# Scattering expert outputs in a two-layer encoder: gate shares by slot, all members summed in one PSUM bank

## The chip, the cores and the metric

One core of a Trainium2 chip runs the whole program. The metric is device time of one execution in microseconds (us). PE is TensorE, DVE VectorE, ACT ScalarE, SP SyncE, which issues the weight transfers.

## The reference

Two post-norm layers over x (256 tokens by 1024). Each has a mixer of three head groups (convolution, differential attention, gated DeltaNet) and a feed-forward part. In layer 1 that part is a mixture of eight experts, of which each token uses two:

```python
logits = t @ router_w
top_v, top_i = lax.top_k(logits, 2)
gates = softmax(top_v)
combine = sum(one_hot(top_i, 8) * gates[..., None], axis=1)
for e in range(8):
    out = out + combine[:, e:e+1] * ((silu(t @ w1[e]) * (t @ w3[e])) @ w2[e])
x = layer_norm(ALPHA * x + out)
```

w1 and w3 of an expert are 1024x3584, w2 is 3584x1024, all in f32.

## The kernel before, in words

**Planner.** The code records instructions, and `Plan.flush` orders each recorded stretch by a list scheduler (`Plan.forward`) with prices of its own. A recorded `E.` operation (class `Either`) goes to ACT, and to DVE only where the planner has ACT busy for more than 6.9 us beyond. After the trunk (everything up to the routing) PE's order is the order of recording (`p.strict`). Each flush ends all engines' lists for that stretch: an instruction of the next stretch stands behind all of this one on its engine. Tiles of one tag have a fixed number of slots, taken in order of recording. ACT and DVE, or PE and either, never touch the same bank and quadrant of PSUM at once: the planner puts a wait between them.

**Experts.** `route` and `places` compute `comb` (the gate shares, token by expert) and `pos` (each token's slot in an expert). Experts are sorted by load into eight places, and `GROUPS` (line 108) makes four groups of them: (0), (2,5), (3,4), (1,6,7). The members' turns over chunks of 512 columns alternate in a group (`TURNS`). In the executions shown each group runs its usual arm, `USUAL_ARMS` (line 113), with so many rows per member: 64; 128 and 64; 128 and 64; 128+64, 32 and 32. A member of 128 rows multiplies in three passes of split operands (fp32r high and low parts of x and of the weights, which ACT casts and DVE subtracts); rows of 64 and 32 ("few") multiply raw f32 in two or four column strips of PE, and their output y lies packed in one bank: strip q of it holds columns q of n of the 1024.

**Weights.** 336 units of 1 MB go through a ring of ten buffers (`RING2`, line 133). SP issues the load of unit u+10 as soon as PE, or the casts, have let unit u go.

**Gather.** `gather` (line 1501) makes one-hot tables `OH` (token by slot) in two blocks of 128 slots, their transposes `oht`, and from them the gathered rows `xe` (16 tiles of 2x128 fp32r columns for each parity of the group). `gather_few` (line 1535) does it for a member of up to 64 rows, into `x64`. The steps for group g+1 are recorded between the turns of group g, one after each turn from the third chunk on (line 1655). Those of group 0 are at the end of the trunk (`before_moe`, line 1673).

**Scatter.** When all turns of a group are done, `Rows.scatter` (line 1860) goes through the members: it splits a bank of y into a high and a low fp32r part (ACT cast, DVE subtraction) in two of the four `mhT` slots, and `Kernel.scatter` (line 1664) multiplies both with the one-hot table of 128 tokens into a bank of tag `pg`, for both token halves t, and adds the bank, times `comb`, into the result `xr` by one DVE instruction. The piece is 512 columns for rows of 128 and of 64, and 256 for rows of 32. So the arms have 4, 8, 8 and 24 such additions. The result of the last group goes straight into `last_norm` (line 1333), on DVE.

**Between groups** each engine takes a branch (`tc.If` on `rare[g]`, line 1723). `HINT` (line 135) puts a mark for the likely next arm so many instructions before the end of each engine's list in the arm: 40 on PE, 10 on ACT, 14 on DVE.

Lines in the profile are nearly all L601 (one place issues all instructions), so groups go by tiles: `bank` is PSUM, `whi`/`wlo`/`parts` are split weights, `xe` or `y` gathered rows, `mhT` the split hidden rows and the split y, `hx` hidden rows of few.

Of the kernel before, what the change touches and what calls it, by code (L numbers as in the profile page):

```python
# [604 lines left out]
class Kernel:  # L605
# [97 lines left out]
    def setup(self, pool):  # L703
# [3 lines left out]
        self.oht = [self.const("oht0", [128, 2, 2, 128], FR)]  # L707
        p.slots("raw", pool, RING, 2048)
# [792 lines left out]
    def gather(self, p, pos, blocks, misc):  # L1501
# [20 lines left out]

        def rows(q, i):
# [8 lines left out]
        return [table] + [lambda q=q, i=i: rows(q, i) for q in range(4) for i in range(2)]  # L1532


    def gather_few(self, p, i, place):
# [13 lines left out]
        def rows():  # L1549
# [6 lines left out]
            self.E.copy(self.x64[p][i], ps)  # L1556

        return [table, rows]

    def gather_group(self, g):  # L1560
# [3 lines left out]
        steps = self.gather(g % 2, self.pos, [(h, C_IOTA), (h, C_IOTA2)], "pg")  # L1564
# [43 lines left out]
    def arm(self, g, *blocks, hint=None):  # L1608
# [8 lines left out]
        if own:  # L1617
            for f in self.gather(1 - p, self.pos, [(GROUPS[g][m], C_IOTA) for m in (own * 2)[:2]], "pg"):
                f()
        members = []  # L1620
        for m, b in enumerate(blocks):
            place = GROUPS[g][m]
            if m and m not in own:
                x, oht = self.x64[p][m - 1], self.oht64[p][m - 1]
                if b == (32,):
                    for r in (32, 96):
                        self.A.copy(oht[r:r + 32], oht[0:32])
                members.append(Rows(self, place, [], [], x[:, :, 0:b[0]], oht))
                continue
            q, at = (1 - p, own.index(m)) if m else (p, 0)  # L1630
            xe, oht = self.xe[q], self.oht[q]
# [3 lines left out]
            if 64 in b:  # L1635
# [4 lines left out]
                few = x, oht[:, n]  # L1640
            members.append(Rows(self, place, xs, ohts, *few))
# [15 lines left out]
        for x in members:  # L1657
            x.scatter()
# [5 lines left out]
    def scatter(self, place, s, oht, y):  # L1664
        for t in range(2):
            ps = self.t("pg", [128, s.stop - s.start])
            self.mm(ps, oht[:, t, :], y[0], True, False)
            self.mm(ps, oht[:, t, :], y[1], False, True)
            self.V.scalar_tensor_tensor(self.xr[:, t, s], ps, self.comb[:, t, place:place + 1], self.xr[:, t, s],
                                        op0=OP.mult, op1=OP.add)  # L1670


    def before_moe(self):
# [10 lines left out]
        for f in self.gather(0, self.slot, [(0, C_IOTA), (0, C_IOTA2)], "pd"):  # L1684
# [3 lines left out]
    def moe(self, pool):  # L1688
        p, nc, tc = self.plan, self.nc, self.tc
        for name, n, words, dt in (("raw2", RING2 - RING, 2048, F32), ("parts", 2, 1024, FR),  # L1690
                                   ("xe", 16, 256, FR), ("oht", 1, 512, FR), ("ohr", 1, 512, FR),
                                   ("mh", 4, 512, F32), ("mhT", 4, 512, FR),
                                   ("td", 8, 16, F32), ("x64", 4, 512, F32), ("oht64", 3, 256, FR),
                                   ("hx", 2, 256, F32)):
# [5 lines left out]
        self.oht.append(self.t("oht", [128, 2, 2, 128], FR, True))  # L1700
# [294 lines left out]
```

## Time and profile before

| | us |
|---|---|
| three runs | 1534.03, 1540.43, 1548.97; median 1540.43 |
| profiled execution | 1527.84 |
| its span, first to last instruction | 1526.1 |
| PE busy | 1414.6 (93%) |
| DVE busy | 822.9 (54%) |
| ACT busy | 585.9 (38%) |
| mean granted PE clock | 0.944 |

The trunk takes the first 628 us; group 0 runs to about 720, group 1 to 955, group 2 to 1186, group 3 to 1512, and the last norm to the end. The clock is a share of 2.4 GHz: 0.50 is 1.2 GHz. A record's duration holds latency; the rate of back-to-back instructions is read from start to start. An f32 matmul leaves two records, an fp32r one of 256 or 512 columns leaves one.

### The profile page before, as it was taken

What the parts mean: (1) busy time and instruction counts of PE and PEld (TensorE: products, weight loads), DVE (VectorE), ACT (ScalarE), POOL (GpSimd) and SP (SyncE); (2) the same over time, 40 slices, a digit from 0 to 9 for tenths busy, and PEclk for the clock granted to TensorE, in tenths of its full rate; (3) what the DMA queues carried; (4) which work ended last, traced back from release to release, by engine and by line L of the source; (5) the groups of instructions that cost most, each with busy time, mean ns of one, the idle gap of its engine ahead of it and who ended that gap; (6) DMA issues with size and microseconds to landing.
All of it is one profiled execution on the core that took longest, in us unless ns stands there. A gap on an engine that the chain in (4) does not pass through costs nothing. (4 is left out here: it accounts for less than half of the span.)

```text
span 1526.1 us, 25192 instructions
## 1 busy us (share of the span) xinstructions
PE 1414.6 (93%) x10040; PEld 1038.4 (68%) x10040; DVE 822.9 (54%) x1669; ACT 585.9 (38%) x969; POOL 16.5 (1%) x33
## 2 busy tenths in 40 slices
PE   8989979999799897898999999999999899999995
PEld 6768769999587676654667666667666666665663
DVE  5995765555769748301555455655454523334346
ACT  4455334444333543211543354444444423323230
POOL 0100000000010000000000000000000000000000
PEclk9988889999899689899899999999999999999997
DMA  8231325455332215599999899899999799999992
GB/s 320 85 136 66 116 100 205 166 193 179 125 111 83 84 56 227 205 421 420 420 420 421 354 373 421 354 413 388 349 372 422 290 420 420 420 420 420 420 419 85
DMA packets 61750, 431.90 MB, mean 283 GB/s; under 512 B 7088, under 2 KB 7856, under 8 KB 10032
## 3 DMA queue, kind: packets, MB, share of 16 engines
q1 hardware_dynamic: 61616, 430.13, 70.4%
q8 instruction: 82, 1.34, 0.4%
q14 instruction: 52, 0.43, 0.1%
HBM read 429.05 MB, written 1.05 MB: 282 GB/s over the span
## 5 line engine op out<-in xcount | busy, mean ns | idle before, releaser
L601 DVE TENSOR_TENSOR wlo<-raw,whi 128x1024 fp32r<-128x1024 f32 x289 | 347.2, 1223 | 356.1 <-ACT whi L601 292.6
L601 ACT CAST whi<-raw 128x1024 fp32r<-128x1024 f32 x289 | 295.7, 1049 | 240.6 <-PE bank L601 196.9
L601 PE MATMUL bank<-raw,x 128*32 128x128 f32 (+1 forms) x3584 | 266.2, 330 | 1.8 <-DVE x L601 1.8
L601 PEld LDWEIGHTS bank<-raw,x 128*32 128x32 f32 (+1 forms) x3584 | 171.2, 124 | 83.8 <-issue 29.6
L601 PE MATMUL bank<-xT,whi 128*128 128x256 f32 x928 | 163.6, 285 | 0.0
L601 PE MATMUL bank<-whi,y 128*128 128x512 f32 x472 | 146.8, 411 | 1.9 <-ACT y L601 0.9
L601 PEld LDWEIGHTS bank<-xT,whi 128*128 128x128 f32 x928 | 138.2, 191 | 5.0 <-ACT L L601 0.8
L601 PE MATMUL bank<-raw,hx 128*64 128x512 f32 (+1 forms) x896 | 131.6, 497 | 0.0
L601 PE MATMUL bank<-whi,xe 128*128 128x512 f32 x336 | 113.0, 418 | 12.2 <-ACT whi L601 9.5
L601 PEld LDWEIGHTS bank<-whi,y 128*128 128x128 f32 x472 | 89.3, 197 | 26.5 <-issue 7.3
L601 PE MATMUL bank<-xT,wlo 128*128 128x256 f32 x464 | 106.3, 285 | 0.8 <-DVE wlo L601 0.8
L601 DVE TENSOR_TENSOR mh<-mh,bank 128x256 f32<-128x256 f32 (+2 forms) x63 | 30.2, 480 | 138.2 <-PE bank L601 138.2
L601 PEld LDWEIGHTS bank<-raw,hx 128*64 128x64 f32 (+1 forms) x896 | 43.7, 125 | 70.3 <-issue 52.0
L601 ACT ACTIVATE mh<-bank 128x256 f32<-128x256 f32 (+2 forms) x63 | 27.2, 432 | 166.1 <-PE bank L601 166.1
L601 PEld LDWEIGHTS bank<-whi,xe 128*128 128x128 f32 x336 | 61.9, 194 | 40.0 <-issue 17.6
L601 PE MATMUL bank<-wlo,y 128*128 128x512 f32 x236 | 85.2, 404 | 3.1 <-DVE wlo L601 3.1
L601 PE MATMUL bank<-whi,mhT 128*128 128x512 f32 x252 | 83.1, 411 | 2.8 <-ACT whi L601 2.8
L601 PE MATMUL bank<-L,raw 128*128 128x256 f32 x352 | 80.5, 386 | 5.4 <-ACT v L601 1.9
L601 PEld LDWEIGHTS bank<-xT,wlo 128*128 128x128 f32 x464 | 78.9, 191 | 3.2 <-DVE wlo L601 1.0
L601 PEld LDWEIGHTS bank<-L,raw 128*128 128x128 f32 x352 | 66.2, 192 | 18.9 <-DVE cpad L601 2.8
L601 DVE TENSOR_TENSOR parts<-raw,parts 128x1024 fp32r<-128x1024 f32 x63 | 76.8, 1218 | 1.7 <-ACT parts L601 1.6
L601 ACT CAST mhT<-bank 128x512 fp32r<-128x512 f32 (+1 forms) x33 | 18.9, 574 | 147.0 <-PE bank L601 146.7
(231 smaller groups left out, 1719.6 us busy)
## 6 DMA issues: line engine op xcount, KB each, us to landing
raw<-in_w SPq DMA_DIRECT2D x400, 1024.0 KB, 10.5
L<-in_row SPq DMA_DIRECT2D x3, 1024.0 KB, 4.6
L<-in_xt SPq DMA_DIRECT2D x2, 512.0 KB, 7.6
raw<-in_w SPq DMA_DIRECT2D x2, 512.0 KB, 8.3
xr<-in_x SPq DMA_DIRECT2D x1, 1024.0 KB, 7.3
raw<-in_row SPq DMA_DIRECT2D x2, 512.0 KB, 7.5
out_y<-xr SPq DMA_DIRECT2D x4, 256.0 KB, 2.1
pw<-in_pw SPq DMA_DIRECT2D x2, 256.0 KB, 4.8
```

What stands on the lines that cost most here:

```text
L601: getattr(self.api[o.eng], o.name)(*[real(x) for x in o.a], **{n: real(x) for n, x in o.k.items()})
```

## The change

The share of a slot (the gate of the token that sits in it) is now computed when the rows are gathered: `shares` multiplies the one-hot table with `comb` into a column, two f32 matmuls of one column for each block, and a DVE copy from PSUM. `gather` gets that as one more step at its end, and `gather_few` does it behind its rows. At the end of a group `Rows.pieces` takes each 256 columns of y times the share (ACT) into a high part and, by one DVE instruction from PSUM, into the low part; both go into the group's own `xe` tiles, which the first products no longer need. `Kernel.scatter` then goes by output piece: four pieces of 256 columns, two token halves, and in each bank all members' high and low products in one accumulation, followed by one DVE addition of 256 columns into `xr`. Each arm so has 8 additions. Where rows of 64 or 32 repeat the one-hot table in other partitions, their shares are copied too (ACT). One slot of tag `td` goes, and `share` tiles come. The diff, whole:

```diff
@@ -705,6 +705,7 @@
         self.pool = pool
         self.slots(pool, True)
         self.oht = [self.const("oht0", [128, 2, 2, 128], FR)]
+        self.share, self.pg = [self.const("share0", [128, 2])], False
         p.slots("raw", pool, RING, 2048)
         self.raws = [self.t("raw", [128, 2048], keep=True) for _ in range(RING)]
         self.xr = self.const("xr", [128, 2, D])
@@ -1498,7 +1499,7 @@
         V.tensor_copy(self.table[:, 2].bitcast(I32), rare)
 
 
-    def gather(self, p, pos, blocks, misc):
+    def gather(self, p, pos, blocks, misc, places):
         A, V, T = self.A, self.V, self.T
         xe, oht = self.xe[p], self.oht[p]
         OH = []
@@ -1520,6 +1521,10 @@
                     T.transpose(pt[:, b, t, :], OH[0][:, t, b, :].bitcast(F32), self.ident)
             A.copy(oht, pt)
 
+        def shares():
+            for b, place in enumerate(places):
+                self.shares(self.share[p][:, b:b + 1], [OH[0][:, t, b, :] for t in range(2)], place)
+
         def rows(q, i):
             ps = self.t(misc, [128, 2, 2, 128])
             for j in range(2):
@@ -1529,7 +1534,7 @@
             for j in range(2):
                 (A.copy if i == 0 else V.tensor_copy)(xe[i][2 * q + j], ps[:, j])
 
-        return [table] + [lambda q=q, i=i: rows(q, i) for q in range(4) for i in range(2)]
+        return [table] + [lambda q=q, i=i: rows(q, i) for q in range(4) for i in range(2)] + [shares]
 
 
     def gather_few(self, p, i, place):
@@ -1554,6 +1559,7 @@
                         self.mm(ps[:, kb, :], self.xh[x][t][:, kb * 128:kb * 128 + 128], OH[0][:, t, 0, :],
                                 kb + t + x == 0, kb + t + x == KB + 1)
             self.E.copy(self.x64[p][i], ps)
+            self.shares(self.share64[p][i], [OH[0][:, t].rearrange("p a b -> p (a b)") for t in range(2)], place)
 
         return [table, rows]
 
@@ -1561,7 +1567,7 @@
         if g >= len(GROUPS):
             return []
         h, *few = GROUPS[g]
-        steps = self.gather(g % 2, self.pos, [(h, C_IOTA), (h, C_IOTA2)], "pg")
+        steps = self.gather(g % 2, self.pos, [(h, C_IOTA), (h, C_IOTA2)], "pg", [h, h])
         for i, place in enumerate(few):
             steps += self.gather_few(g % 2, i, place)
         return steps
@@ -1615,20 +1621,22 @@
         self.psum_tags({"py": ny, "pg": 8 - ny})
         steps, own = self.gather_group(g + 1), [m for m, b in enumerate(blocks) if 128 in b and m]
         if own:
-            for f in self.gather(1 - p, self.pos, [(GROUPS[g][m], C_IOTA) for m in (own * 2)[:2]], "pg"):
+            mine = [GROUPS[g][m] for m in (own * 2)[:2]]
+            for f in self.gather(1 - p, self.pos, [(place, C_IOTA) for place in mine], "pg", mine):
                 f()
         members = []
         for m, b in enumerate(blocks):
-            place = GROUPS[g][m]
             if m and m not in own:
                 x, oht = self.x64[p][m - 1], self.oht64[p][m - 1]
+                share = self.share64[p][m - 1]
                 if b == (32,):
                     for r in (32, 96):
                         self.A.copy(oht[r:r + 32], oht[0:32])
-                members.append(Rows(self, place, [], [], x[:, :, 0:b[0]], oht))
+                        self.A.copy(share[r:r + 32], share[0:32])
+                members.append(Rows(self, [], [], [], x[:, :, 0:b[0]], oht, share))
                 continue
             q, at = (1 - p, own.index(m)) if m else (p, 0)
-            xe, oht = self.xe[q], self.oht[q]
+            xe, oht, share = self.xe[q], self.oht[q], self.share[q]
             full = [at + n for n in range(b.count(128))]
             xs = [lambda kb, n=n, xe=xe: [xe[i][kb][:, n, :] for i in range(2)] for n in full]
             ohts, few = [oht[:, n] for n in full], ()
@@ -1637,8 +1645,9 @@
                 for kb in range(KB):
                     self.V.tensor_tensor(x[:, kb, :], xe[0][kb][:, n, 0:64], xe[1][kb][:, n, 0:64], OP.add)
                 self.A.copy(oht[64:128, n], oht[0:64, n])
-                few = x, oht[:, n]
-            members.append(Rows(self, place, xs, ohts, *few))
+                self.A.copy(share[64:128, n:n + 1], share[0:64, n:n + 1])
+                few = x, oht[:, n], share[:, n:n + 1]
+            members.append(Rows(self, xs, ohts, [share[:, n:n + 1] for n in full], *few))
         alone = len(members) == 1
         for n, (m, k, ch) in enumerate(turns):
 
@@ -1654,20 +1663,34 @@
                 members[m].second(ch)
             if steps and ch >= 2 and not own:
                 steps.pop(0)()
-        for x in members:
-            x.scatter()
+        self.scatter(p, members)
         for f in steps:
             f()
         self.plan.flush(hint)
 
 
-    def scatter(self, place, s, oht, y):
+
+    def scatter(self, p, members):
+        room = [x.rearrange("p a b -> p (a b)") for part in self.xe[p] for x in part]
+        while members:
+            n = next(n for n in range(len(members), 0, -1) if sum(x.tiles() for x in members[:n]) <= len(room))
+            tiles, now, members = iter(room), members[:n], members[n:]
+            found = [y for x in now for y in x.pieces(tiles)]
+            for q in range(4):
+                mine, s = [y[1:] for y in found if y[0] == q], slice(256 * q, 256 * q + 256)
+                for t in range(2):
+                    ps = self.t("pg", [128, 256])
+                    for i, (oht, *parts) in enumerate(mine):
+                        for k, y in enumerate(parts):
+                            self.mm(ps, oht[:, t, :], y, i + k == 0, i == len(mine) - 1 and k == 1)
+                    self.V.tensor_tensor(self.xr[:, t, s], ps, self.xr[:, t, s], OP.add)
+
+
+    def shares(self, out, OH, place):
+        ps = self.t("pg" if self.pg else "pd", [128, 1])
         for t in range(2):
-            ps = self.t("pg", [128, s.stop - s.start])
-            self.mm(ps, oht[:, t, :], y[0], True, False)
-            self.mm(ps, oht[:, t, :], y[1], False, True)
-            self.V.scalar_tensor_tensor(self.xr[:, t, s], ps, self.comb[:, t, place:place + 1], self.xr[:, t, s],
-                                        op0=OP.mult, op1=OP.add)
+            self.mm(ps, OH[t].bitcast(F32), self.comb[:, t, place:place + 1], t == 0, t == 1)
+        self.V.tensor_copy(out, ps)
 
 
     def before_moe(self):
@@ -1681,7 +1704,7 @@
 
             self.E.mul(self.xr[:, t, :], self.xr[:, t, :], ALPHA)
         self.bias("gather")
-        for f in self.gather(0, self.slot, [(0, C_IOTA), (0, C_IOTA2)], "pd"):
+        for f in self.gather(0, self.slot, [(0, C_IOTA), (0, C_IOTA2)], "pd", [0, 0]):
             f()
         self.plan.bias = 0.0
 
@@ -1690,14 +1713,16 @@
         for name, n, words, dt in (("raw2", RING2 - RING, 2048, F32), ("parts", 2, 1024, FR),
                                    ("xe", 16, 256, FR), ("oht", 1, 512, FR), ("ohr", 1, 512, FR),
                                    ("mh", 4, 512, F32), ("mhT", 4, 512, FR),
-                                   ("td", 8, 16, F32), ("x64", 4, 512, F32), ("oht64", 3, 256, FR),
-                                   ("hx", 2, 256, F32)):
+                                   ("td", 7, 16, F32), ("x64", 4, 512, F32), ("oht64", 3, 256, FR),
+                                   ("hx", 2, 256, F32), ("share", 4, 2, F32)):
             p.slots(name, pool, n, words, dt)
         first = [self.raws[u % RING] for u in range(M0, M0 + RING)]
         self.raws2 = first + [self.t("raw2", [128, 2048], keep=True) for _ in range(RING2 - RING)]
         self.parts.append([self.t("parts", [128, 1024], FR, True) for i in "hl"])
         self.xe.append([[self.t("xe", [128, 2, 128], FR, True) for kb in range(KB)] for i in "hl"])
         self.oht.append(self.t("oht", [128, 2, 2, 128], FR, True))
+        self.share.append(self.t("share", [128, 2], keep=True))
+        self.share64, self.pg = [[self.t("share", [128, 1], keep=True) for _ in range(n)] for n in (1, 2)], True
         self.x64 = [[self.t("x64", [128, KB, 64], keep=True) for _ in range(n)] for n in (1, 2)]
         self.oht64 = [[self.t("oht64", [128, 2, 128], FR, True) for _ in range(n)] for n in (1, 2)]
         for u in range(M0 + RING, M0 + RING2):
@@ -1782,8 +1807,9 @@
 
 
 class Rows:
-    def __init__(self, k, place, xs, ohts, few=None, oht_few=None):
-        self.k, self.place, self.xs, self.ohts, self.few, self.oht_few = k, place, xs, ohts, few, oht_few
+    def __init__(self, k, xs, ohts, shares, few=None, oht_few=None, share_few=None):
+        self.k, self.xs, self.ohts, self.shares = k, xs, ohts, shares
+        self.few, self.oht_few, self.share_few = few, oht_few, share_few
         self.ys = [[k.t("py", [128, 512]) for _ in range(2)] for _ in xs]
         if few:
             m = few.shape[2]
@@ -1857,18 +1883,29 @@
                              ch == NCHUNK - 1 and f == 3)
             o.streamed()
 
-    def scatter(self):
-        o, s = self.k, [slice(0, 512), slice(512, 1024)]
-        for y, oht in zip(self.ys, self.ohts):
-            for hf in range(2):
-                yh, yl = o.t("mhT", [128, 512], FR), o.t("mhT", [128, 512], FR)
-                o.split(yh, yl, y[hf])
-                o.scatter(self.place, s[hf], oht, (yh, yl))
+
+
+    def pieces(self, tiles):
+        o, found = self.k, []
+
+        def parts(x, share):
+            hi, lo = next(tiles), next(tiles)
+            o.E.affine(hi, x, share)
+            o.V.scalar_tensor_tensor(lo, x, share, hi, op0=OP.mult, op1=OP.subtract)
+            return hi, lo
+
+        for y, oht, share in zip(self.ys, self.ohts, self.shares):
+            for q in range(4):
+                found.append((q, oht, *parts(y[q // 2][:, q % 2 * 256:q % 2 * 256 + 256], share)))
         if self.few:
-            yh, yl = [o.t("mhT", [128, 1024 // self.n], FR) for _ in range(2)]
-            o.split(yh, yl, self.y)
-            for q, r in enumerate(self.rows):
-                o.scatter(self.place, self.cols(1024, q), self.oht_few[r], (yh[r], yl[r]))
+            n = 4 // self.n
+            for c in range(n):
+                hi, lo = parts(self.y[:, 256 * c:256 * c + 256], self.share_few)
+                found += [(n * j + c, self.oht_few[r], hi[r], lo[r]) for j, r in enumerate(self.rows)]
+        return found
+
+    def tiles(self):
+        return 8 * len(self.ys) + (8 // self.n if self.few else 0)
```

## Rows read from the trace of the kernel before

**Rows 1.** Windows of 25 us, MoE; DMA share, GB/s last
```profile
850.00:875.00 25.00, 25.00 (x129) 17.21 (x129) 8.93 (x8) 7.50 (x9) 0.00 (x0) 0.89 0.85 330
...
950.00:975.00 25.00, 21.20 (x94) 14.84 (x93) 17.73 (x21) 12.05 (x14) 0.00 (x0) 0.86 0.86 328
...
1175.00:1200.00 25.00, 21.13 (x93) 12.53 (x93) 16.84 (x27) 12.19 (x17) 0.00 (x0) 0.86 0.63 259
```

**Rows 2.** Timeline, TensorE, where group 1 ends (start, duration, instruction, idle before)
```profile
950.24 2.54 PE L601 MATMUL bank<-mhT,oht 128*128 128x512 f32 x9
953.07 1.39 PE L601 MATMUL bank<-mhT,oht 64*128 64x512 f32 x7 [0.29 <-DVE mhT L601]
954.88 0.70 PE L601 MATMUL bank<-whi,y 128*128 128x512 f32 x2 [0.42 <-issue]
958.68 0.80 PE L601 MATMUL bank<-wlo,y 128*128 128x512 f32 x1 [3.09 <-DVE wlo L601]
959.27 1.05 PE L601 MATMUL bank<-whi,y 128*128 128x512 f32 x2
...
965.31 1.55 PE L601 MATMUL bank<-parts,y 128*128 128x512 f32 x6
```

**Rows 3.** Timeline, VectorE, then ScalarE, same place
```profile
951.01 1.41 DVE L601 SCALAR_TENSOR_TENSOR xr<-bank,comb,xr 128x512 f32<-128x512 f32 x2 [2.94 <-PE bank L601]
...
952.93 4.03 DVE L601 SCALAR_TENSOR_TENSOR xr<-bank,comb,xr 128x512 f32<-128x512 f32 x6
956.88 0.61 DVE L601 TENSOR_SCALAR ohr<-m,pos 128x256 fp32r<-128x256 f32 x2
957.40 3.49 DVE L601 TENSOR_TENSOR wlo<-raw,whi 128x1024 fp32r<-128x1024 f32 x3
...
951.24 0.59 ACT L601 CAST mhT<-bank 128x512 fp32r<-128x512 f32 x1 [3.89 <-PE bank L601]
```

**Rows 4.** Timeline, VectorE, where group 2 ends
```profile
1187.21 1.16 DVE L601 TENSOR_TENSOR x<-xe,xe 128x64 f32<-128x64 f32 x8
1188.29 3.48 DVE L601 TENSOR_TENSOR wlo<-raw,whi 128x1024 fp32r<-128x1024 f32 x3
```

**Rows 5.** Timeline, VectorE, then ScalarE, where group 0 ends
```profile
726.95 0.62 DVE L601 TENSOR_SCALAR ohr<-m,pos 128x256 fp32r<-128x256 f32 x2 [4.21 <-issue]
...
723.97 2.94 ACT L601 CAST whi<-raw 128x1024 fp32r<-128x1024 f32 x3 [5.27 <-issue]
```

**Rows 6.** Timeline, TensorE, then VectorE, end of the kernel
```profile
1497.50 3.33 PE L601 MATMUL bank<-mhT,oht 128*128 128x512 f32 x10
...
1504.96 6.75 PE L601 MATMUL bank<-mhT,oht 32*128 32x256 f32 x28 [0.36 <-DVE xr L601]
...
1512.14 1.27 DVE L601 BATCH_NORM_STATS2 td<-xr 128x6 f32<-128x512 f32 x2
```

**Rows 7.** Windows of 2 us in the last scatter, PEclk third from the end
```profile
1502.00:1504.00 2.00, 1.88 (x8) 0.91 (x7) 2.00 (x4) 0.37 (x1) 0.00 (x0) 1.00 0.00 0
1504.00:1506.00 2.00, 1.64 (x7) 1.34 (x8) 1.90 (x5) 0.00 (x0) 0.00 (x0) 0.54 0.00 0
```

**Rows 8.** Groups of instructions, all of the kernel, by form
```profile
L601 DVE TENSOR_TENSOR mh<-mh,bank 128x256 f32<-128x256 f32 x28 | 11.8, 420 | 68.6 <-PE bank L601 68.6
...
L601 DVE SCALAR_TENSOR_TENSOR xr<-bank,comb,xr 128x256 f32<-128x256 f32 x16 | 7.1, 481 | 0.4
...
L601 ACT CAST y<-bank 128x256 fp32r<-128x256 f32 x16 | 5.1, 380 | 8.2 <-PE bank L601 8.2
...
L601 ACT ACTIVATE c<-bank,sm 128x256 f32<-128x256 f32 x4 | 2.0, 561 | 4.7 <-PE bank L601 4.7
```

**Rows 9.** Timeline, TensorE, in the trunk
```profile
431.86 1.05 PE L601 MATMUL bank<-cmisc,d 128*128 128x2 f32 x8
...
438.07 0.40 PE L601 MATMUL bank<-xT,whi 128*128 128x256 f32 x2
...
438.43 0.40 PE L601 MATMUL bank<-xT,whi 128*128 128x256 f32 x2
```

## The prediction

> **What bounds the kernel now.** I read the experts' part first by windows of 25 us. The reader is to see that TensorE is busy 25.00 of 25 us while the transfers fall to 0.85 of their capacity, so in groups 1 and 2 PE sets the pace and the ring is full; and that at the ends of groups 1 and 2 both fall together (PE to 21 us, transfers to 0.86 and 0.63) [rows 1]. Time that PE loses there is lost to the transfers too, which later run without a gap until the last unit. So a microsecond gained or lost on PE before about 1190 us moves the end by about as much, and the end itself is a chain of scatter and norm.
>
> Then the timelines of the three places where scatters end. At the end of group 1, PE's last second-product ends where the scatter starts, at 950.24; the additions hold DVE from 951.01 to 956.88, a table takes 0.5 us more, and the first `wlo` of the next group, begun at 957.40, lets PE go on at 958.68 after 3.09 us of idling [rows 2, 3]. DVE, not PE, ends this stage. The second member's split starts only at 951.24, a microsecond after its y is complete, since its `mhT` slot is still read by the scatter of the first member [rows 3]. Group 2 ends alike: additions up to 1187.21, eight `x` additions, `wlo` at 1188.29 [rows 4]. At the end of group 0 DVE and ACT stand 4.21 and 5.27 us for nothing the profile shows, at the branch [rows 5]. At the kernel's end the scatter runs from 1497.50 to 1512.14, where the norm's first instruction starts [rows 6]: 14.6 us in which no weight moves [rows 7].
>
> **The tail.** Before, 8 additions of 512 and 16 of 256 columns go one after the other on DVE (0.48 us each for the latter [rows 8]). They go. What is late next is PE: each of 8 banks takes four members' high and low parts, 64 matmuls of 256 columns. The trunk's dense run has three such matmuls from 438.07 to 438.43, so 0.12 us each at full clock [rows 9] (those of 32 rows took 0.24 at half clock [rows 6], so fewer rows save nothing). The parts of the first member, and those of the second, are made while PE still multiplies for the third, since the `xe` tiles are free by then. Only the third's are late: a high part (ACT, 0.38 us [rows 8]) and a low part (DVE, 0.48). A hand-over costs 0.2 to 0.3 us, an estimate from the first addition of before: two matmuls of 0.23 us from 950.24, and DVE begins at 951.01 [rows 2, 3]. That makes 1497.50 + 0.2 + 0.4 + 0.15 + 0.45 + 0.25 = 1498.95; by then PE has done the first six. The other 58 take 7.0 us, until 1505.9; the last addition (0.42 us, as the same form on `mh` [rows 8]) ends at 1506.5. Against 1512.1: **-5.6 us**. The bounds: the high part with its scale from a tile may take the 0.56 us of the nearest row with such an operand [rows 8], worth 0.2; the matmuls take 0.24 us at half clock (28 in 6.75 us [rows 6]), which is rival B.
>
> **Ends of groups 1 and 2.** The planner keeps ACT and DVE from one bank at a time, so for the second member (one bank, two pieces) come two high parts and then two low parts: 950.24 + 0.2 + 0.75 + 0.15 + 0.48 + 0.25, so PE goes on at 952.1, having done two matmuls. 30 more at 0.12 us end at 955.7, and the last addition at 956.3, against 956.88 before: -0.6. The same for group 2. Together **-1.2 us** (bounds: 0.9 more, were the low parts not behind both high ones; nothing, were the high part 0.56).
>
> **The clock there.** Rows show PE at 1.2 GHz after the 3.09 us of idling: 15 matmuls of 512 columns from 959.27 to 965.31, 0.40 us each, and then six in 1.55, 0.26 each [rows 2]. The excess is 15 x 0.15 = 2.3 us; the window's mean clock of 0.86 says the same [rows 1]. In the changed kernel the idle time is cut in two: 1.6 us ahead of the parts, then dense matmuls, then some 2.3 us with two matmuls in them. I take it that the fall doesn't come at one of the two places: **-2.3 us** (bounds 0 and -4.6). Of this the Trainium skill, "TensorE: Matmul & The Clock Gate" (Part 1), says that the half rate is the resting state and that activity lifts it; the trace agrees in that the clock fell in the last scatter, to 0.54, when PE waited for every addition [rows 7]. By that rule alone, with less idling at both ends, both falls would go (rival C).
>
> **What the shares add.** Two f32 matmuls of one column a block: two records each, and eight records of the nearest kind (128x128 weights, two columns) take 1.05 us [rows 9], so 0.13 a record at most; I take 0.11. In group 0's arm 12 records, in group 1's 12, in group 2's 16, and 8 in the trunk. In groups 1 and 2 PE is the pace, so 28 x 0.11 = **+3.1 us** (bounds 0, if transfers hide it, and 3.6). In group 0 matmuls already wait for transfers: 0. In the trunk the 8 records and two copies come behind the last gathered rows: **+0.4** (0 to 1.0). The copies of shares into other partitions are on ACT, which has time; the DVE copies of one column stand in a queue where DVE is half idle (8.9 to 14.5 us of 25 [rows 1]) and hold only a `pg` bank, of which groups 1 and 2 have five: 0. At the end of group 0 four additions of 512 columns become eight of 256, the same time: 0 (0.5 either way). The lost `td` slot concerns tiles that one engine writes and reads: 0.
>
> **The sum.** -5.6 - 1.2 - 2.3 + 3.1 + 0.4 = -5.6 us: from the profiled execution's 1527.8 to 1522.2 us. The median of the runs shown lies 12.6 us above that execution; the same difference taken from 1540.4 gives **1534.8 us**. About 1% is what a measurement of this kernel can tell from no change, and this is 0.4%.
>
> **Rivals.**
> A. *The branch is no longer covered* (slower). Marks for the next arm stand 40, 10 and 14 instructions before the end of a list. The scatter now has 32 matmuls instead of 16 in groups 1 and 2, so on PE the mark comes at the start of the last member's products, about 9 us ahead of the branch instead of about 12. From under the 4.2 to 5.3 us of idling seen at group 0's end [rows 5] it would fail. Then DVE goes on at 956.3 + 4.2 = 960.5 instead of 956.88, +3.6 at each of two places, and no clock is saved: 3.1 + 0.4 + 7.2 - 5.6 = +5.1, 1545.5 us. For it speaks that the mark fails at group 0; against it, that it holds in groups 1 and 2 and keeps 4 us in hand. The Trainium skill, "Runtime: NRT & Kernel Launch" (Instruction fetch mechanics), says that a taken branch to a page not at hand stalls for its fetch. By that rule every end would stall; the trace agrees at one end of three. Chance 0.13.
> B. *The scatters run at half clock.* PE now waits at the start of each scatter. At 0.24 us a matmul the tail ends at 1498.95 + 13.9 + 0.6 = 1513.5 (+1.3), and the ends of groups 1 and 2 at 959.9 (+3.0 each): 1.3 + 6.0 + 3.5 = +10.8, 1551.2. Against it: the clock stood at 1.00 until 1504 while PE waited more than it will now [rows 7]. Chance 0.07.
> C. *No fall of the clock at either end*: 2.3 more, 1532.5. Chance 0.13.
> D. *Transfers hide the middle*: if groups 1 to 3 are bound by the ring after all, shares and ends cost and give nothing; only the tail and the trunk are left: -5.2, 1535.2. For it: full transfer rate in most windows between the dips; against it the 0.85 with PE full [rows 1]. Chance 0.14.
> E. *The planner orders the trunk anew.* The new instructions behind `comb` lengthen the remaining path of what leads to it by about a microsecond, and all the trunk is planned in one stretch of 628 us. Nothing in the profile gives the size; I allow 8 us either way. Chance 0.13.
> The forecast itself has 0.40.
>
> **Range and chances.** A, C, D and the forecast lie from 1532 to 1546; B and E reach to 1526 and 1551, and the three runs shown lie 15 us apart. So 1523 to 1550. Faster by over 1% (below 1525) needs E and C together or a low median: 0.09. Slower by over 1% (above 1555.8) needs B and E: 0.06. Within: 0.85.
>
> **What would show it.** Right: the norm's first statistics about 9 us behind the start of the scatter instead of 14.6; 64 matmuls of 256 columns at 0.12 us with the clock at 1.00; DVE's additions of 0.42 us never waiting for each other; at group 1's end `wlo` half a microsecond earlier relative to 950.24; about 0.9 us of new records per gather. Wrong: idling for "issue" at the ends of groups 1 and 2, a granted clock of 0.50 in a scatter, a trunk longer or shorter than 628 us by more than 1 us, or an end of group 2 that moved by more than 4 us.

## The result, and the profile after

The changed kernel is slower: 1553.81 us median (1541.01 to 1577.26, 19 runs) against 1535.68 of the kernel before beside it (1527.23 to 1550.23, 19 runs), a ratio of 1.0118 with a 95% interval of 1.0093 to 1.0143. The forecast was 1534.8 us, 0.4% faster. Executions of either kernel fall into groups some 8 to 20 us apart, and the ratios leave out those more than 1.5% above their kernel's fastest, so a ratio also depends on which groups were met: the same kernel gave 1.0037 in later runs (below). The stages of a profiled execution, read from start to start, are steadier, and the reasons rest on them.

The profiled execution has a span of 1549.6 us, 23.5 more than before. Each stage runs from the first matmul of its kind to that of the next: "end of group" from the scatter's first matmul to the next group's first `wlo` matmul, the tail from the scatter to the norm's first statistics, and the norm to VectorE's last instruction. The last column is the experiment e10 below.

| stage, us | before | after | after, 2nd execution | with order and mask |
|---|---|---|---|---|
| start to routing | 609.1 | 609.5 | 611.5 | 609.3 |
| routing to group 0's first product | 19.34 | 24.70 | 20.50 | 20.48 |
| group 0 | 90.28 | 94.87 | 93.34 | 93.33 |
| end of group 0 | 10.01 | 7.74 | 7.61 | 7.64 |
| group 1 | 221.48 | 223.55 | 222.07 | 221.44 |
| end of group 1 | 8.44 | 12.99 | 10.94 | 8.07 |
| group 2 | 221.88 | 221.89 | 224.06 | 224.11 |
| end of group 2 | 9.00 | 12.94 | 12.78 | 8.75 |
| group 3 | 307.94 | 309.12 | 309.46 | 307.83 |
| tail | 14.64 | 18.09 | 17.98 | 11.40 |
| norm | 10.65 | 10.89 | 10.90 | 10.91 |

Both executions of the changed kernel lose at the ends of groups 1 and 2 and in the tail, where the forecast had its gains, and in group 0, where it had nothing.

The end of group 1 on TensorE and then VectorE, which answer to [rows 2, 3] (start, duration, instruction, idle time before):

```profile
960.39 1.03 PE L601 MATMUL bank<-xe,oht 128*128 128x256 f32 x3
961.92 8.43 PE L601 MATMUL bank<-xe,oht 64*128 64x256 f32 x29 [0.50 <-DVE xe L601]
970.28 1.22 PE L601 MATMUL bank<-whi,y 128*128 128x512 f32 x2
973.38 0.80 PE L601 MATMUL bank<-wlo,y 128*128 128x512 f32 x1 [1.88 <-DVE wlo L601]
```

```profile
962.34 0.43 DVE L601 TENSOR_TENSOR xr<-bank,xr 128x256 f32<-128x256 f32 x1
963.20 0.42 DVE L601 TENSOR_TENSOR xr<-bank,xr 128x256 f32<-128x256 f32 x1 [0.43 <-PE bank L601]
...
968.95 0.42 DVE L601 TENSOR_TENSOR xr<-bank,xr 128x256 f32<-128x256 f32 x1 [1.02 <-PE bank L601]
970.39 0.42 DVE L601 TENSOR_TENSOR xr<-bank,xr 128x256 f32<-128x256 f32 x1 [1.02 <-PE bank L601]
972.11 3.49 DVE L601 TENSOR_TENSOR wlo<-raw,whi 128x1024 fp32r<-128x1024 f32 x3
```

The reader is to see two things. TensorE is named as busy for 8.43 us with 29 matmuls, 0.29 us each; the forecast had 0.12. And VectorE, which had set this stage before, now waits for a bank ahead of each addition but the first. A bank takes four matmuls, so the distance of two additions is the price of four: 0.86 us at first, 1.45 once the clock has fallen.

The tail, TensorE then VectorE (answer to [rows 6]), and 2-us windows in it (answer to [rows 7]; engines' busy time and records in the order PE, PEld, DVE, ACT, POOL, then the granted clock, DMA share, GB/s):

```profile
1517.33 17.71 PE L601 MATMUL bank<-xe,oht 128*128 128x256 f32 x64
```

```profile
1518.96 0.42 DVE L601 TENSOR_TENSOR xr<-bank,xr 128x256 f32<-128x256 f32 x1 [0.48 <-PE bank L601]
1520.48 0.42 DVE L601 TENSOR_TENSOR xr<-bank,xr 128x256 f32<-128x256 f32 x1 [1.09 <-PE bank L601]
...
1532.48 0.42 DVE L601 TENSOR_TENSOR xr<-bank,xr 128x256 f32<-128x256 f32 x1 [2.17 <-PE bank L601]
1535.08 0.42 DVE L601 TENSOR_TENSOR xr<-bank,xr 128x256 f32<-128x256 f32 x1 [2.17 <-PE bank L601]
1535.42 1.27 DVE L601 BATCH_NORM_STATS2 td<-xr 128x6 f32<-128x512 f32 x2
```

```profile
1518.00:1520.00 2.00, 2.00 (x12) 1.46 (x12) 0.91 (x2) 0.00 (x0) 0.00 (x0) 1.00 0.04 8
1520.00:1522.00 2.00, 2.00 (x12) 1.37 (x11) 0.42 (x1) 0.00 (x0) 0.00 (x0) 0.93 0.00 0
1522.00:1524.00 2.00, 2.00 (x7) 1.55 (x7) 0.42 (x1) 0.00 (x0) 0.00 (x0) 0.50 0.00 0
```

The 64 matmuls were there as forecast, but eight of a bank take 1.52 us even at clock 1.00, 0.19 each, and 2.60 at 0.50. The rows show PE "busy" 2.00 of 2.00 us as the clock falls, though 12 matmuls at 0.12 us would fill only 1.4 of them: a busy time holds latency. Busy shares hide the loss: PE stands at 93% of the span before and after.

By the groups by form no one size is slow: those of 128, 64 and 32 rows all have a mean record of about 0.4 us (the last line is the shares, used below). A bank's matmuls differ in size in one thing only, the rows they use:

```profile
L601 PE MATMUL bank<-xe,oht 64*128 64x256 f32 x32 | 10.9, 425 | 0.6 <-DVE xe L601 0.5
L601 PE MATMUL bank<-xe,oht 128*128 128x256 f32 x32 | 10.4, 415 | 0.0
L601 PE MATMUL bank<-xe,oht 32*128 32x256 f32 x32 | 8.4, 398 | 0.0
L601 PE MATMUL bank<-comb,ohr 128*128 128x1 f32 x48 | 7.5, 265 | 0.2 <-DVE share L601 0.2
```

The end of group 0 has the same size of matmul, two to a bank, but 64 rows throughout, and runs at 0.11 us each:

```profile
729.99 1.67 PE L601 MATMUL bank<-y,oht 64*128 64x256 f32 x15 [0.50 <-DVE y L601]
```

So neither the 256 columns nor 64 rows by themselves cost. That gives the theory: **a change of the row count from one matmul to the next costs**, by the distances above (0.86 - 4 x 0.12) / 2 = 0.19 us at full clock. The changed kernel has two such changes per bank at the ends of groups 1 and 2 (128, 64, and 128 again for the next bank) and three in the tail (128, 64, 32); the kernel before finished one row count ahead of the next. The Trainium skill, "TensorEngine Tiling (Array Packing)" (Tiling Modes, Key Properties), says that changing the tiling mode, not just the tile, drains TensorE. It gives no price; the trace agrees with 0.19 us. Single records of the first execution show where some of it goes: a matmul behind a change begins with its weight load (both at 962.23 us), while the next one, of the same count, has its load begun 0.11 us ahead of itself (962.34 and 962.46), under the matmul before it.

### The profile page after: what moved, and what is told of

It reads as the page before. It is cut to its first block, busy times and chain, and to the rows that moved or that the text cites. A ratio compares the mean times of both kernels' runs of the same rounds, so it can differ in the third digit from the quotient of the medians.

```text
span 1549.6 us, 25402 instructions
## 1 busy us (share of the span) xinstructions
PE 1440.6 (93%) x10144; PEld 1062.9 (69%) x10144; DVE 814.6 (53%) x1679; ACT 589.0 (38%) x985; POOL 16.5 (1%) x33
## 5 line engine op out<-in xcount | busy, mean ns | idle before, releaser
L601 PE MATMUL bank<-wlo,xe 128*128 128x512 f32 x168 | 69.6, 414 | 6.1 <-DVE wlo L601 6.1
```

The lines of the kernel that those rows point to most:

```text
L601: getattr(self.api[o.eng], o.name)(*[real(x) for x in o.a], **{n: real(x) for n, x in o.k.items()})
```

## Experiments

**e1, the order.** Two banks are open at a time, the token half is the inner loop, and every other piece takes the members backwards, so that equal row counts meet.

```diff
-                for t in range(2):
-                    ps = self.t("pg", [128, 256])
-                    for i, (oht, *parts) in enumerate(mine):
+                banks = [self.t("pg", [128, 256]) for t in range(2)]
+                for i, (oht, *parts) in enumerate(mine[::-1] if q % 2 else mine):
+                    for t, ps in enumerate(banks):
```

> The changed kernel with another order of the scatter's matmuls alone: two banks (both token halves) open at once, the members' shapes taken from 128 rows down to 32 and back up in the next piece. Theory S (a matmul whose operands lie in another number of partitions than those of the matmul before costs about 0.2 us more at full clock and 0.3 at half, and the gaps then let the clock fall): such changes of shape fall from 15 to 4 in each scatter of groups 1 and 2 and from 23 to 8 in the last, so some 2 to 3 us less at the ends of groups 1 and 2, 4 to 9 us less in the tail, ratio to before about 1.003 to 1.007 instead of 1.012. Rival R (256 columns a matmul, with many products added up in one bank, cost 0.2 us or more whatever the order): scatter as long as in the changed kernel, 18 us in the tail, ratio 1.012.

Measured: ratio 1.0011 [0.9966, 1.0055], below the range expected. End of group 1 8.60 us, of group 2 9.04, the tail 14.70: the 4 us at each end are back, more than the 2 to 3 expected, and the tail gained 3.4, less than the 4 to 9. It ran at half clock from 1520 on and so only drew level with before. The end of group 1 on TensorE, with four changes in the scatter instead of 15 and 0.15 us a matmul instead of 0.29:

```profile
964.01 4.01 PE L601 MATMUL bank<-xe,oht 64*128 64x256 f32 x27 [0.50 <-DVE xe L601]
```

**e2, one row count.** Members of few rows go through their table in all 128 partitions. This leaves out the separation of the strips, so the output isn't the layer's; the matmuls are as many as in the changed kernel, all of one row count.

```diff
-                found += [(n * j + c, self.oht_few[r], hi[r], lo[r]) for j, r in enumerate(self.rows)]
+                found += [(n * j + c, self.oht_few, hi, lo) for j, r in enumerate(self.rows)]
```

> The changed kernel, but rows of 64 and 32 are multiplied in all 128 partitions, so that no matmul of a scatter changes the shape; this adds wrong strips to the output, so part of the computation is changed, with the same count of matmuls and columns. Theory S: 0.11 to 0.12 us from matmul to matmul, clock at 1.00 in the scatters, about 9 us from the start of the last scatter to the norm's first statistics, ratio to before 1.002 to 1.005. Rival R: 0.2 us a matmul, ratio 1.012.

Measured: ratio 0.9963 [0.9920, 1.0006], below the 1.002 to 1.005 expected; but the medians of all runs give 1.0023, and the profiled execution spent 625.0 us up to the routing instead of 609.5, which the scatter has no part in. So the ends count here: 8.20, 9.28 and 8.62 us. The tail (TensorE, then VectorE, then a window of 2 us):

```profile
1523.34 8.24 PE L601 MATMUL bank<-xe,oht 128*128 128x256 f32 x64
```

```profile
1525.92 0.42 DVE L601 TENSOR_TENSOR xr<-bank,xr 128x256 f32<-128x256 f32 x1 [0.52 <-PE bank L601]
1526.86 0.42 DVE L601 TENSOR_TENSOR xr<-bank,xr 128x256 f32<-128x256 f32 x1 [0.52 <-PE bank L601]
```

```profile
1527.00:1529.00 2.00, 2.00 (x19) 2.00 (x18) 0.94 (x3) 0.00 (x0) 0.00 (x0) 1.00 0.00 0
```

The same 64 matmuls, in the same order and banks, take 8.24 us instead of 17.71: 0.94 a bank, 0.12 a matmul, at clock 1.00. This is the tail that the forecast had described (9 us); that all members share a bank costs nothing.

**e9, twice as many changes.** All members' first parts, then all members' second parts: the same matmuls, four changes a bank instead of two, and six instead of three in the tail.

```diff
-                    for i, (oht, *parts) in enumerate(mine):
-                        for k, y in enumerate(parts):
-                            self.mm(ps, oht[:, t, :], y, i + k == 0, i == len(mine) - 1 and k == 1)
+                    for k in range(2):
+                        for i, (oht, *parts) in enumerate(mine):
+                            self.mm(ps, oht[:, t, :], parts[k], i + k == 0, i == len(mine) - 1 and k == 1)
```

> The changed kernel with the two loops inside a bank exchanged: all members' first parts, then all members' second parts. The same matmuls with the same rows, but the number of rows changes 4 times a bank instead of 2 at the ends of groups 1 and 2, and 6 times instead of 3 in the tail. Theory that a change of the row count costs 0.2 us at the full clock and 0.3 at half: from the last product's end to the next stage 4 to 5 us more at the ends of groups 1 and 2 (about 17 instead of 13), 6 to 7 more in the tail (about 25 instead of 18), in all about 15 us, and a ratio 0.010 above that of the changed kernel run as it is. Rival, that the matmuls of few rows are slow by themselves or that the wait for the bank sets the pace: the three ends stay at 13, 13 and 18 within 1 us.

Measured: ratio 1.0194 [1.0120, 1.0268] (4 runs), and 17.09, 17.48 and 25.20 us at the three ends. VectorE's additions at the end of group 1, two at full clock and two at half, and two in the tail:

```profile
977.61 0.42 DVE L601 TENSOR_TENSOR xr<-bank,xr 128x256 f32<-128x256 f32 x1 [0.82 <-PE bank L601]
978.86 0.42 DVE L601 TENSOR_TENSOR xr<-bank,xr 128x256 f32<-128x256 f32 x1 [0.83 <-PE bank L601]
...
986.47 0.42 DVE L601 TENSOR_TENSOR xr<-bank,xr 128x256 f32<-128x256 f32 x1 [1.61 <-PE bank L601]
988.51 0.42 DVE L601 TENSOR_TENSOR xr<-bank,xr 128x256 f32<-128x256 f32 x1 [1.62 <-PE bank L601]
...
1562.79 0.42 DVE L601 TENSOR_TENSOR xr<-bank,xr 128x256 f32<-128x256 f32 x1 [3.06 <-PE bank L601]
1566.27 0.42 DVE L601 TENSOR_TENSOR xr<-bank,xr 128x256 f32<-128x256 f32 x1 [3.06 <-PE bank L601]
```

A bank takes 1.25 us against 0.86 at full clock, 2.04 against 1.45 at half, 3.48 against 2.60 in the tail. The matmuls are the same and the changes two or three more, so one costs 0.39 / 2 = 0.19 us at full clock, and 0.59 / 2 = 0.30 or 0.88 / 3 = 0.29 at half: three differences, and no price of a matmul assumed. One thing besides differs: each matmul now has another one-hot table than the one before it. e11 has that too, at no cost.

**e11, changes of strip alone.** In group 0's scatter the 64-row matmuls alternate between partitions 0 to 63 and 64 to 127 (by the edit 15 changes of strip, not 14). The rest is the kernel of e8 below.

```diff
+                for pair in (0, 2), (1, 3):
...
+                            for q in pair:
+                                self.mm(banks[q, t], by[q][1][:, t, :], by[q][2 + k], k == 0, k == 1)
```

> As the kernel with halved shares, but in group 0's scatter (one member, all matmuls of 64 rows) the matmuls go alternately to the strip of partitions 0 to 63 and to that of 64 to 127: 14 changes of the strip in 16 matmuls instead of one, and no change of the number of rows. There the last 15 matmuls take 1.68 us. Theory that only a change of the number of rows costs: 1.7 to 1.9 us again for the 16th part and the rest alike. Rival, that any change of the rows in use costs 0.2 us at the full clock: 13 more changes, 2.6 us, so about 4.3 us for the same matmuls.

Measured, in one profiled execution; first the same scatter in e8, then here:

```profile
728.64 1.68 PE L601 MATMUL bank<-y,oht 64*128 64x256 f32 x15 [0.50 <-DVE y L601]
```

```profile
723.86 0.38 PE L601 MATMUL bank<-y,oht 64*128 64x256 f32 x2 [0.60 <-ACT y L601]
724.75 1.40 PE L601 MATMUL bank<-y,oht 64*128 64x256 f32 x14 [0.50 <-DVE y L601]
```

14 matmuls in 1.40 us, 0.10 each: another strip of the same size costs nothing. It is the count that costs, as the sentence of the Trainium skill on mode and tile has it ("TensorEngine Tiling (Array Packing)", Tiling Modes, Key Properties). The single records show more: the two strips' matmuls start in pairs, less than 0.01 us apart, and the pairs 0.12 apart (724.97, 725.09, 725.21), so two strips of one size run at the same time.

**e3, shares alone.** The shares are made as in the change and the scatter is that of before.

```diff
-        self.scatter(p, members)
+        for x in members:
+            x.scatter()
```

> The gather side of the change alone: shares are computed and copied as in the changed kernel, but the scatter is that of before and multiplies with the gate at the addition, so the shares are not used. Theory G (the shares cost more than 3.5 us, since they stand in front of the first product of the experts and their one-column matmuls let the clock fall): 5 to 9 us, ratio 1.003 to 1.006, and group 0 begins about 2 us later counted from the routing's first DVE copy. Rival as predicted: 3.5 us, ratio 1.002; rival hidden: 1.000.

Measured: ratio 1.0044 [1.0008, 1.0079], 6.8 us. The ends are those of before (9.88, 8.44, 8.99, 14.63). Routing to first product 20.51 (+1.2), group 0 93.44 (+3.2), group 1 +2.0; group 2 took 228.74, 6.9 more, with 17 us inside it at half clock instead of 3.4. Whether the shares bring that on is open: group 2 took 221.9 and 224.1 in the changed kernel, which has them too, and 228.6 and 229.0 in e1 and e6, which also have them.

**e4, the scatter alone.** No shares; the parts are a plain split of y, so the gate is left out.

```diff
-            o.E.affine(hi, x, share)
-            o.V.scalar_tensor_tensor(lo, x, share, hi, op0=OP.mult, op1=OP.subtract)
+            o.split(hi, lo, x)
```

> The scatter side of the change alone: no shares are computed, and the parts are y itself, split into high and low, so the gate is left out of the output. Theory S: the scatters at the ends of groups 1 and 2 and of the kernel are as long as in the changed kernel, together about 12 us longer than before, ratio 1.005 to 1.008. Rival (the shares make all of the loss): ratio 0.996 to 1.000.

Measured: ratio 1.0016 [0.9978, 1.0055], under the 1.005 to 1.008 expected. Group 0 is back (90.72), the slow ends stay (13.69, 12.51, 17.82): scatter and shares are separate costs. Group 1 took 214.94, 6.5 less than before, with no fall of the clock inside; why is open. It keeps this kernel's whole time from showing the ends' 12 us.

**e6, the shares' matmuls three times.**

```diff
-        for t in range(2):
-            self.mm(ps, OH[t].bitcast(F32), self.comb[:, t, place:place + 1], t == 0, t == 1)
+        for again in range(3):
+            for t in range(2):
+                self.mm(ps, OH[t].bitcast(F32), self.comb[:, t, place:place + 1], t == 0, t == 1)
```

> e3_shares_only with each share's matmuls made three times over (the scatter is that of before). Theory G (these one-column matmuls stand on PE's path and let the clock fall): 8 us or more above e3_shares_only's 1.0044, group 0 some 5 us longer than e3's 93.4. Rival (the loss of e3 comes from the wait and copies at the start of the experts, or from chance): at most 3 us more, ratio 1.004 to 1.006.

Measured: ratio 1.0189 [1.0124, 1.0255] (6 runs). The records' group in e3 and here:

```profile
L601 PE MATMUL bank<-comb,ohr 128*128 128x1 f32 x48 | 8.1, 278 | 0.2 <-DVE share L601 0.2
...
L601 PE MATMUL bank<-comb,ohr 128*128 128x1 f32 x144 | 19.0, 261 | 0.2 <-DVE share L601 0.2
```

10.9 us more for 96 records, 0.11 each. Group 0 rose by 6.7 to 100.18 where its 24 additional records make 2.6: the rest is clock, 6.8 us at half in its first part where the shares alone have 3.4, and more behind it. Groups 1, 2 and 3 hardly moved (+0.7, +0.2, -0.3), though groups 1 and 2 have 24 and 32 records more.

**e5 and e10, order and mask.** e1's order, and for the 64-row members two tables in an idle tile that are zero outside their strip, so that groups 1 and 2 have 128 rows throughout.

```diff
+                self.A.activation(tables[:, j], self.m128[:, C_IOTA:C_IOTA2 + 1, :], AF.Copy, scale=0.0)
+                self.A.copy(tables[r, j], x.oht_few[r])
...
+                found += [(n * j + c, self.whole[j], hi, lo) if self.whole else
+                          (n * j + c, self.oht_few[r], hi[r], lo[r]) for j, r in enumerate(self.rows)]
```

> The order of e1_order, and the rows of 64 multiplied in all 128 partitions with two one-hot tables that are zero outside their strip (made by ACT in the idle one-hot tile, before the scatter), so the output stays whole. Theory S: no change of shape in the scatters of groups 1 and 2 and about 4 in the last; 8.2 and 9.2 us from the scatter's start to the first matmul with the next low weights (12.99 and 12.94 in the changed kernel), 9 to 11 us from the last scatter's start to the norm (18.1), ratio to before 0.996 to 1.001. Rival (the zero tables or the fuller matmuls cost as much as they save): ratio 1.001 or more, as e1_order.

> The kernel with order and mask once more, beside the one with half the records. It gave 0.9978 with an interval of 0.9943 to 1.0013. If its three ends are what it gains (8, 8.9 and 10.8 us against 8.4, 9.0 and 14.6, less about 3 in group 0), the ratio is 0.997 to 0.999 again; if the first ratio was a matter of which executions fell where, it comes out at 1.000 or above.

Measured: 0.9978 [0.9943, 1.0013] and 0.9940 [0.9901, 0.9978]. The ends are 8.07, 8.91 and 10.75, then 8.07, 8.75 and 11.40. The second ratio lies below the range expected of it. The profiled spans (1527.8 and 1526.5) equal that of before, so the gain in the median can't be placed in a stage.

**e7, late shares.** As e5, with the shares of groups 0 and 3 made inside their own group instead of ahead of it.

```diff
+        if g in LATER:
+            steps.pop()
```

> e5_order_mask, and the shares of groups 0 and 3 are made inside their own group, not at the end of the trunk and in group 2. Theory G: from the routing to the first product 19.3 us again or 1 to 5 us less than e5, group 2 some 2 us shorter, group 3 no longer since it waits for transfers; ratio 2 to 5 us under e5, about 0.994 to 0.998. Rival: the start of the experts is set by the clock's phase and not by the shares: same ratio as e5.

Measured: 0.9993 [0.9954, 1.0032]; group 0 92.80, group 2 219.42 (224.03 in e5), tail 11.19. From the routing to the first product it took 23.53, not 19.3 or less: the longer way there that the first execution of the changed kernel had (24.70) came here without a share in the trunk. No gain over e5 can be told.

**e8, half the records.** As e5; a share is one rounded matmul of two columns (head and rest) per half.

```diff
-            self.mm(ps, OH[t].bitcast(F32), self.comb[:, t, place:place + 1], t == 0, t == 1)
-        self.V.tensor_copy(out, ps)
+            self.mm(ps, OH[t], self.combs[:, t, place, :], t == 0, t == 1)
+        self.V.tensor_reduce(out, ps, AX.X, OP.add)
```

> As the kernel with order and mask, but a share is now made of half the matmul records: the shares' column is kept once per launch as two rounded columns (a head and a rest), one rounded matmul takes both, and VectorE adds the two results as it takes them out of the bank. Theory that the shares cost by their records on TensorE (tripling them cost 6.6 us in group 0 and about 1 in each part behind): group 0 falls by 1 to 2 us from 93.3 and the ratio is 2 to 4 us under that of the kernel with order and mask run beside it, about 0.996. Rival, that what is left is the chain of an eviction and a multiplication per strip on the other engines, whatever TensorE does: no stretch moves by over 0.5 us for it, and the two ratios agree.

Measured: 0.9933 [0.9893, 0.9972], 1531.70 us against 1543.45; beside it e10 gave 0.9940, so the two can't be told apart. Group 0 falls by 0.66 us to 92.67 for 6 records less (0.11 each, 1.8 to 1.0 us busy); the 1 to 2 us expected were too many.

**The changed kernel again.**

> The changed kernel itself once more, beside the others on one chip: ratio 1.007 to 1.014, scatters of 13, 13 and 18 us.

Measured: 1549.50 against 1538.54, ratio 1.0037 [1.0007, 1.0067], below the range expected; that of the medians is 1.0071. Span 1544.4. The sign holds, the size lies between 0.4 and 1.2%. The end of group 2 and the tail are again 12.78 and 17.98; at group 1 it is 10.94, not 13, with all eight additions 0.86 apart: the clock didn't fall there this time.

## Why the prediction was wrong

**The tail (forecast -5.6; measured +3.4).** The step that failed is the price of a matmul: "three such matmuls ... 0.12 us each at full clock [rows 9] (those of 32 rows took 0.24 at half clock [rows 6], so fewer rows save nothing)". Both rows come from runs of one row count; the change mixes three in each bank. Eight matmuls and three changes make 0.96 + 3 x 0.19 = 1.53 us, and 1.52 was measured at full clock. 23 changes at 0.19 are 4.4 of the 9.0 us between forecast and result; the rest is half clock from about 1522 on, the fall of rival B. The count of matmuls and the last addition's place were right: without changes (e2) the tail took 8.62 us. The 0.24 at half clock was no price of TensorE's either: VectorE, with an addition of 0.48 for every two matmuls, set that pace. By 2.60 = 8 x 0.215 + 3 x 0.29 a matmul takes 0.215 at half clock.

**Ends of groups 1 and 2 (forecast -1.2 for both and -2.3 for the clock; measured +4.5 at one and +3.9 at the other).** The same step. Instead of "30 more at 0.12 us end at 955.7", 29 took 8.43 us. Of this 29 matmuls at 0.12 are 3.5 and 15 changes at 0.19 are 2.9; the other 2.0 are **the clock**, as the second execution shows, whose clock stood at 1.00 there:

```profile
956.53 6.38 PE L601 MATMUL bank<-xe,oht 64*128 64x256 f32 x29 [0.50 <-DVE xe L601]
```

The clock was taken as won and in fact lost: rival B's half clock came, in the second half of each of these scatters in the first execution, and in the second execution at group 2. Around the two ends TensorE stood at half clock for 13.6 us before, and for 23.9 and 13.6 in the two executions, so no fall was saved. B was given 0.07 because PE would wait less. PE did wait little by the rows, but it did 4.6 instead of 8 matmuls in a microsecond. B's price for the tail, +1.3, lacked the changes; that its total of 1551.2 lies near the measured median is chance.

**Shares.** "In group 0 matmuls already wait for transfers: 0" failed: group 0 cost 4.6 and 3.1 us. The three costliest groups of TensorE and the shares in group 0, before and then in e10 (its 3.1 us are free of the further fall that the first execution had):

```profile
L601 PE MATMUL bank<-raw,x 128*64 128x256 f32 x448 | 53.5, 391 | 1.8 <-DVE x L601 1.8
L601 PE MATMUL bank<-raw,hx 128*64 128x512 f32 x112 | 25.5, 597 | 0.0
```

```profile
L601 PE MATMUL bank<-raw,x 128*64 128x256 f32 x448 | 55.1, 399 | 1.8 <-DVE x L601 1.8
L601 PE MATMUL bank<-raw,hx 128*64 128x512 f32 x112 | 25.5, 597 | 0.0
...
L601 PE MATMUL bank<-comb,ohr 128*128 128x1 f32 x12 | 1.8, 269 | 0.0
```

TensorE's only idle time there is 1.8 us at the start: it isn't transfers that set group 0, so the 12 records cost in full, 1.3 us at 0.11 each (their busy time of 1.8 overlaps its neighbours'). The other 1.6 are on `raw,x`, one stretch of 3.4 us at half clock at the group's start, just behind the routing and its shares. The price per record was right (0.11 taken, 0.11 by e8 and by e6). The sum for groups 1 and 2 came close, +3.1 forecast and +2.1 and +2.8 measured, but that is luck as far as is known: in e6 56 records more, 6.2 us at the price, added 0.9 there, and single groups vary by more than either. The trunk's +0.4 was +1.2 in the second execution and in e10, and +5.4 in the first, where the routing ran longer at half clock.

**The branch (rival A).** It stayed covered at the ends of groups 1 and 2: VectorE goes on to the next group 0.8 and 0.7 us behind the last addition, not the 4.2 of the rival. At the end of group 0 the 4.21 us of [rows 5] are gone on VectorE (its tables follow the last addition without idling) and remain on ScalarE (5.07 idle), and 2.3 us are gained, where 0 was taken. Why VectorE is now in time wasn't tried.

**The order of the trunk (E), and transfers hiding the middle (D).** Start to routing took 609.5 and 611.5 against 609.1: no re-ordering of the size allowed. D falls with e9: its ends of groups 1 and 2 are 4.1 and 4.5 us longer than in the changed kernel, and groups 2 and 3 behind them took 221.7 and 310.7 against 221.9 and 309.1, so no transfer hid it.

**The median.** The forecast moved the median by the difference of stages. Its spread, and that of the ratios (1.0118 and 1.0037 for one kernel), comes at least in part from falls of the clock that differ between executions: up to the routing e2 and e9 have the work of the changed kernel, and their profiled executions took 625.0 and 623.1 us at a mean clock of 0.89 against 609.5 at 0.91. The range of 1523 to 1550 ended below the 1551.2 of rival B, the one case in which several stretches lose clock together.

## What to carry to other kernels

Matmuls with different numbers of rows should be issued in runs of one count, or the few rows padded by a table that is zero elsewhere: each change cost 0.19 us at 2.4 GHz and 0.30 at 1.2, more than the matmul of 256 columns (0.12) itself. A duration from a dense run holds only for a run of that shape; ask for each new sequence what differs from one instruction to the next. With order, mask and cheaper shares (e8) the change gave 0.9933 [0.9893, 0.9972] of the time before; but the four comparisons of kernels with order and mask (e5, e7, e8, e10) lie between 0.9933 and 0.9993, and their profiled spans (1526.5 to 1528.1 us) are no shorter than that of before, so a gain is likely and small, and no stage shows it.

## What the runs showed of the hardware

- A change of the row count between matmuls costs 0.19 us (full clock) or 0.30 (half); a change of strip with the same count costs nothing, and the matmuls of two strips run in pairs (0.10 us a matmul in e11).
- TensorE's clock fell to 0.50 (1.2 GHz) in a stretch that the profile calls 100% busy (12 records in 2 us), and stayed at 1.00 where as many matmuls came dense (e2: 8.24 us for 64). The Trainium skill, "TensorE: Matmul & The Clock Gate" (Part 1), says that activity lifts the rate; the trace agrees as far as the dense stretch kept it. It didn't fall each time: in the second execution the 29 matmuls at the end of group 1 ran at 1.00.
- An f32 matmul of one column costs about 0.11 us a record (e6, e8), as much as an fp32r one of 256 in a dense stretch (0.12, e2). Each has a weight load of its own in the rows; whether that sets the price wasn't tried.
